# Four feed-forward stages of a hybrid decoder, issued in written order on every engine

## The chip, the cores and the metric

One core of one Trainium2 chip runs the whole program. The metric is the device time of one execution in microseconds (us); several runs are taken and their median is given. The profile comes from one further execution, with the hardware profiler on.

## What is computed

The input is 512 tokens of 1024 features in float32. Two layers follow one another, each a feed-forward block, a mixer (gated linear attention in the first layer, stick-breaking attention in the second) and another feed-forward block; a norm ends it. The change concerns the feed-forward blocks alone, of which there are four:

```
def rmsnorm(x, g):
    y = xf * lax.rsqrt(jnp.mean(xf * xf, axis=-1, keepdims=True) + EPS)
    return (y * g.astype(jnp.float32)).astype(x.dtype)

def swiglu(h, w_gate, w_up, w_down):
    return (jax.nn.silu(h @ w_gate) * (h @ w_up)) @ w_down

x = x + 0.5 * swiglu(rmsnorm(x, ffn1_norm[i]), ffn1_w_gate[i], ffn1_w_up[i], ffn1_w_down[i])
```

The gate and up weights are 1024 x 2816, the down weights 2816 x 1024.

## The kernel before

**Layout.** The residual stays in SBUF as eight tiles xs of 128 features x 512 tokens. Every float32 matrix product is made of three matmuls: each operand is cut into a high part (a cast by ScalarE, `wh`, `hh`, `nh`, `th`, `xh`) and a low part (VectorE subtracts the high part from the original: `wl`, `hl`, `nl`, `tl`, `xl`), and TensorE adds up high x high, high x low and low x high (`mm3`, L63 for the matmuls themselves).

**The feed.** All the work that needs weights stands in one list, `feed.q`, of entries. An entry has the weight units that it needs and a body with its matmuls and what empties them. `Feed.start` takes the next entry e. It first cuts the weights of e and of the entries behind it, up to three entries and four units of 128 x 1024 in all (`Entry.split`, cast in L134, subtraction in L135), then asks for the loads of e and the five entries behind it (SyncE, L114), then runs the body. `feed.entries(n)` starts n entries one after another. Of the cut weights there are four buffers each for high and low, of the loaded gate and up chunks (`raw`, 1 MB) two, of the loaded down chunks (`rawd`, 0.5 MB) two.

**A feed-forward stage** is one `FFN`. The 2816 columns are taken in 11 column blocks of 256 (c = 0 to 10), in six groups. Blocks 0 and 1 use plain products (`feat`), and so does the gate half of block 2. All others use a scheme of seven half-size products in place of eight (`seven`), which I call a block of seven products; each column block from 3 on has one for the gate weights and then one for the up weights. A block is two entries:

- `body_1` runs four products, into banks w, z, q and w again. Behind the first ScalarE copies w into `u` (L579). Behind the second VectorE adds z into `u` (L555), behind the third ScalarE copies q into `c` (L586), and behind the fourth the first half of an output o is made (`left`): by SiLU on ScalarE in a gate block, by a product with the gate on VectorE in an up block (L561).
- `body_2` runs three products, into the other half of z, onto q, and into the other half of w. VectorE adds (L555, L599); a gate block ends in two SiLUs (`rest`, L565), an up block in two products with the gate (L568), each of which is then cut into high and low for the down product (`close`: cast in L630, subtraction in L631).

The units of a block are partly sums of pieces of the loaded weights, made by VectorE while the weights are cut: two additions for `body_1` (`sums_12`, L529 and L530) and two for `body_2` (`sums_34`, L535 and L536). The programs below call all of these `s`.

Down entries (`down`, 24 matmuls each, emptied into xs by VectorE in L309) of the group before are put between the blocks: one behind each block of seven in column blocks 3 to 7, two in block 8, one each behind the up blocks of 9 and 10, and two ahead of the up block of 2. The last group's four come at the end.

At the start of a stage the plain entries are interleaved with `normed_input` (four pieces which scale, cut and difference the input) and then `sums` (eight pieces which cut the differences); `FFN.run` writes them between the calls of `feed.entries`.

**What sets the order.** The program is traced, and a scheduler at the end orders each engine's instructions by its own estimate of when they become ready, so an engine's queue can differ from the written order. Within `tc.manual_schedule()` it doesn't: there each engine issues in the order in which the program was written. Before the change only the opening of the whole kernel and a few lines of the first stage (L696 to L699) stand in such a block. An engine works through its queue in order either way: what is written behind a waiting instruction waits too. The data dependencies, the buffers and the waits for them are worked out by the framework for both.

Of the kernel before, what the change touches and what calls it, by code (L numbers as in the profile page):

```python
# [31 lines left out]
def decoder(ctx: ExitStack, tc: tile.TileContext, a: dict, out: bass.AP):  # L32
    nc = tc.nc
# [12 lines left out]
    def psum(name, tag=None):  # L46
        if tag is None:
            tag = order[turn_[0] % 8]
            turn_[0] += 1
        return pp.tile([P, T], F32, tag=tag, bufs=banks[tag], name=name)  # L50
# [11 lines left out]
    def mm(ps, l, r, first, last):  # L62
        st["pe"] = nc.tensor.matmul(ps, l, r, start=first, stop=last).ins  # L63
# [8 lines left out]
    def four(m):  # L72
        return m.rearrange("p (h t n) -> p t n h", h=2, t=2)
# [4 lines left out]
    def quads(ps):  # L78
        return ps.rearrange("p (t n h) -> p t n h", t=2, h=2)
# [99 lines left out]
    feed = Feed()  # L179
# [163 lines left out]
    st = {}  # L343
# [64 lines left out]
    def stats_b(tag=None, turned=False):  # L408

        ps = psum("ps_R", tag)  # L410
        dgs = sp.tile([P, T], F32, tag="ss", name="dg")
        for i in range(NT):
            dg = dgs[:, i * P : (i + 1) * P]
            nc.vector.tensor_scalar(
                out=dg, in0=ident, scalar1=st["r4"][:, i : i + 1], scalar2=None, op0=ALU.mult
            )
            mm(ps[:, i * P : (i + 1) * P], ones, dg, True, True)
        st["R"] = sp.tile([P, T], F32, tag="sq", name="R")
        nc.vector.tensor_copy(st["R"], ps)
        if turned:  # L420
            st["Rq"] = sp.tile([P, T], F32, tag="Rq", name="Rq")
            nc.vector.tensor_copy(quads(st["Rq"]), four(ps))

    def two_halves(between=None, n=2):

        feed.finish()
        g = [feed.start() for _ in range(n)]
        for i in range(3):
            for x in g:
                next(x, None)  # L430
            if i == 0 and between is not None:
                between()

    def new_norm():
        st["h"], st["l"] = st["nh"], st["nl"]

    def flush(deferred):
        for evac, ps in deferred:
            evac(ps)
        deferred.clear()  # L440
# [11 lines left out]
    class FFN:  # L452
# [235 lines left out]
        def run(self, between=None):  # L688
            with tc.tile_pool(name="hp", bufs=8, reuse_waits="tile") as self.hp, tc.tile_pool(
                name="tp", bufs=5, reuse_waits="tile"  # L690
            ) as self.tp:
                st["few"] = self.hp
                new_norm()

                if self.first:
                    with tc.manual_schedule():  # L696
                        feed.entries(1)
                        stats_b(turned=True)
                        flush(self.defer)  # L699
                else:  # L700
                    two_halves(stats_a)
                    stats_b(turned=True)
                    flush(self.defer)
                done = feed.pos - self.base
                for job, n in ((self.normed_input, self.NORMED - done), (self.sums, self.sums_by - self.NORMED)):
                    todo = list(job())
                    for i in range(n):
                        for piece in todo[i * len(todo) // n : (i + 1) * len(todo) // n]:
                            piece()
                        feed.entries(1)  # L710
                    self.normed = True
                    st["h"], st["l"] = zip(*self.n)
                feed.entries(self.count - self.sums_by)
                if between is not None:
                    with tc.issue_after(st["silu"]):
                        nc.scalar.preload_act_table_set("sqrt_and_others")
                    feed.q[feed.pos].split()
                    between(self.tp)
                feed.entries(self.total - self.count)


    class GLA:
# [764 lines left out]
```

## Time and profile before

| what | value |
|---|---|
| median of 3 runs | 1817.53 us (1817.35 to 1818.69) |
| the profiled execution: its time | 1816.56 us |
| the profiled execution: span from first to last instruction | 1814.8 us |
| busy share of TensorE, VectorE, ScalarE | 99%, 81%, 51% |
| mean granted TensorE clock | 0.998 |

The profile calls the engines PE (TensorE matmuls), PEld (TensorE weight loads), DVE (VectorE), ACT (ScalarE), POOL (GpSimd) and SP (SyncE). A row of a group names the line, the engine, the operation and the tiles as out<-in, with the numbers of buffers left out, then the count, the busy time, the mean duration of one, and the idle time of the engine ahead of them with what ended it. The four feed-forward stages lie at about 0 to 345, 575 to 907, 910 to 1235 and 1480 to 1815 us of the span; the two mixers between them.

### The profile page before, as it was taken

How to read it: one execution, taken by the hardware profiler on the slowest of the kernel's cores; microseconds unless marked ns; L12 is line 12 of the kernel's file. 1: busy time of each engine (PE TensorE's matmuls, PEld its weight loads, DVE VectorE, ACT ScalarE, POOL GpSimd, SP SyncE). 2: the span in 40 equal slices, each digit the busy share in tenths (PEclk: the TensorE clock that was granted, in tenths of full speed). 3: DMA queues.
4: the chain of work that ended last, by engine and by line, in shares of the span. 5: the costliest groups of instructions: out<-in, count | busy, mean ns of one | idle time of the engine just before them, and what ended most of it. 6: DMA issues, size and time to landing. Idle time of an engine off the chain costs nothing.

```text
span 1814.8 us, 28968 instructions
## 1 busy us (share of the span) xinstructions
PE 1794.2 (99%) x11806; PEld 1640.7 (90%) x11806; DVE 1473.1 (81%) x2373; ACT 926.2 (51%) x1455; POOL 8.5 (0%) x20
## 2 busy tenths in 40 slices
PE   9999999999999999999999999999999999999998
PEld 7899999889988899999989999999888788999997
DVE  7988887776877988887898888787888779888785
ACT  6444435445554544444554444455888844444444
POOL 0000000100000000000000000000000000000000
PEclk9999999999999999999999999999999999999999
DMA  6243333212223323332233333233221223333321
GB/s 210 72 131 112 105 117 114 84 51 67 70 70 102 107 94 112 113 125 84 82 119 119 110 116 106 89 96 96 70 71 59 70 93 116 105 105 105 120 90 70
DMA packets 177608, 179.09 MB, mean 99 GB/s; under 512 B 4098, under 2 KB 167988, under 8 KB 177476
## 3 DMA queue, kind: packets, MB, share of 16 engines
q1 hardware_dynamic: 176224, 175.13, 29.9%
q8 instruction: 92, 1.51, 0.3%
q0 software_dynamic: 576, 1.05, 0.2%
q10 hardware_dynamic: 676, 1.07, 0.2%
q14 instruction: 40, 0.33, 0.1%
HBM read 175.17 MB, written 2.10 MB: 98 GB/s over the span
## 4 chain that ended last, share of the span: by engine, by line
PE 85%; DVE 8%; ACT 4%; DMA 3%; issue 1%; DVEq 0%; ACTq 0%; SPq 0%
PE ps_d L63 23%; PE ps_w L544 14%; PE ps_f L63 14%; PE ps_z L544 9%; PE ps_q L544 9%; PE ps_t L63 4%; PE ps_b L63 3%; DVE wl L135 2%; PE ps_S L63 1%; DMA raw<-in_ffn_w_up_dram 1%; PE ps_bt L63 1%; PE ps_oT L1176 1%; PE ps_z L1114 1%; DMA raw<-in_ffn_w_gate_dram 1%; ACT wh L134 1%
## 5 line engine op out<-in xcount | busy, mean ns | idle before, releaser
L135 DVE TENSOR_TENSOR wl<-raw,wh 128x1024 fp32r<-128x1024 f32 x242 | 258.2, 1068 | 50.4 <-ACT wh L134 49.7
L134 ACT CAST wh<-raw 128x1024 fp32r<-128x1024 f32 (+1 forms) x242 | 223.8, 927 | 130.0 <-PE ps_f L63 43.4
L63 PE MATMUL ps_d<-hh,wh 128*128 128x512 f32 x672 | 254.7, 379 | 0.0
L63 PE MATMUL ps_d<-hh,wl 128*128 128x512 f32 x672 | 254.7, 379 | 0.0
L63 PE MATMUL ps_d<-hl,wh 128*128 128x512 f32 x672 | 254.7, 379 | 0.0
L134 ACT CAST wh<-s 128x1024 fp32r<-128x1024 f32 x136 | 142.3, 1046 | 115.0 <-PE ps_q L544 82.0
L135 DVE TENSOR_TENSOR wl<-s,wh 128x1024 fp32r<-128x1024 f32 x136 | 165.8, 1219 | 23.9 <-ACT wh L134 22.7
L63 PE MATMUL ps_f<-xh,wh 128*128 128x512 f32 x456 | 178.7, 392 | 3.4 <-DVE x L243 1.7
L63 PE MATMUL ps_f<-xh,wl 128*128 128x512 f32 x456 | 173.8, 381 | 0.4 <-DVE wl L1366 0.4
L63 PE MATMUL ps_f<-xl,wh 128*128 128x512 f32 x456 | 173.6, 381 | 0.0
L309 DVE SCALAR_TENSOR_TENSOR x<-ps_d,x 128x512 f32<-128x512 f32 x184 | 124.6, 685 | 59.8 <-PE ps_d L63 59.7
L544 PE MATMUL ps_z<-th,wh 128*128 128x256 f32 x544 | 150.1, 276 | 0.3 <-DVE u L555 0.2
L544 PE MATMUL ps_w<-nh,wl 128*128 128x256 f32 x544 | 149.6, 275 | 0.0
L544 PE MATMUL ps_w<-nl,wh 128*128 128x256 f32 x544 | 149.6, 275 | 0.0
L544 PE MATMUL ps_z<-th,wl 128*128 128x256 f32 x544 | 149.6, 275 | 0.0
L544 PE MATMUL ps_z<-tl,wh 128*128 128x256 f32 x544 | 149.6, 275 | 0.0
L544 PE MATMUL ps_w<-nh,wh 128*128 128x256 f32 x544 | 149.5, 275 | 0.0
L134 ACT CAST wh<-rawd 128x1024 fp32r<-128x1024 f32 x84 | 88.0, 1048 | 120.4 <-PE ps_d L63 100.7
L63 PEld LDWEIGHTS ps_d<-hl,wh 128*128 128x128 f32 x672 | 127.0, 189 | 18.0
L63 PEld LDWEIGHTS ps_d<-hh,wl 128*128 128x128 f32 x672 | 127.2, 189 | 16.5
L63 PEld LDWEIGHTS ps_d<-hh,wh 128*128 128x128 f32 x672 | 127.2, 189 | 16.5
L135 DVE TENSOR_TENSOR wl<-rawd,wh 128x1024 fp32r<-128x1024 f32 x84 | 102.6, 1222 | 34.7 <-ACT wh L134 34.4
(268 smaller groups left out, 4711.0 us busy)
## 6 DMA issues: line engine op xcount, KB each, us to landing
raw<-in_ffn_w_gate_dram SPq DMA_DIRECT2D x43, 1024.0 KB, 5.1
raw<-in_ffn_w_up_dram SPq DMA_DIRECT2D x43, 1024.0 KB, 5.1
rawd<-in_ffn_w_down_dram SPq DMA_DIRECT2D x84, 512.0 KB, 3.5
raw<-in_gla_w_in_dram SPq DMA_DIRECT2D x12, 1024.0 KB, 5.3
raw<-in_sb_w_in_dram SPq DMA_DIRECT2D x16, 512.0 KB, 3.8
raw<-in_gla_w_out_dram SPq DMA_DIRECT2D x4, 1024.0 KB, 5.1
raw<-in_sb_w_in_dram SPq DMA_DIRECT2D x4, 1024.0 KB, 5.0
raw<-in_sb_w_out_dram SPq DMA_DIRECT2D x4, 1024.0 KB, 4.9
```

Of the source, the lines that this page charges most:

```text
L63: st["pe"] = nc.tensor.matmul(ps, l, r, start=first, stop=last).ins
L134: nc.scalar.copy(h, r).ins,
L135: nc.vector.tensor_tensor(out=l, in0=r, in1=h.bitcast(F32), op=ALU.subtract).ins,
L309: nc.vector.scalar_tensor_tensor(out=x, in0=back_by(ps, 4), scalar=0.5, in1=x, op0=ALU.mult, op1=ALU.add)
L544: nc.tensor.matmul(pairs(o), l_, r_, start=first and j + n == 0, stop=j == 3 and n == 2, skip_group_check=True)
L1114: nc.tensor.matmul(o_, l_, r_, start=first, stop=last, skip_group_check=True)
L1176: nc.tensor.matmul(po[e * 64 : e * 64 + 64, j * P : T], self.v[j][:, c : c + 64], self.wt[p, e][bk][:, c0 : c0 + n], start=j == 0, stop=j ...
```

## The change

`FFN.run` now opens `tc.manual_schedule()` for the whole of the first stage, and in the other three from behind the first two entries and the norm; it is closed behind the last entry of the stage. In the last stage the load of the square-root table loses its `issue_after`, since the written order already puts it behind the last SiLU. Nothing is computed otherwise.

```
+                self.es = ExitStack()
                 if self.first:
-                    with tc.manual_schedule():
-                        feed.entries(1)
-                        stats_b(turned=True)
-                        flush(self.defer)
+                    self.es.enter_context(tc.manual_schedule())
+                    feed.entries(1)
+                    stats_b(turned=True)
+                    flush(self.defer)
                 else:
                     two_halves(stats_a)
                     stats_b(turned=True)
                     flush(self.defer)
+                    self.es.enter_context(tc.manual_schedule())
...
                 if between is not None:
-                    with tc.issue_after(st["silu"]):
-                        nc.scalar.preload_act_table_set("sqrt_and_others")
+                    nc.scalar.preload_act_table_set("sqrt_and_others")
                     feed.q[feed.pos].split()
                     between(self.tp)
                 feed.entries(self.total - self.count)
+                self.es.close()
```

The instructions of every engine are the same. TensorE's order differs at a few places, at the starts of the stages; that of VectorE and ScalarE differs all through the stages, that of SyncE a little.

First place: VectorE, an up block of seven products in the middle of the first stage, from the product with the gate (L561) to the second cut (L631). The o are the block's two outputs, u and c its helpers, s the sums of weights. Before:

```order
L561 TENSOR_TENSOR o_1785<-ps_w,o_1626 128x256
L135 TENSOR_TENSOR wl<-s_1844,wh 128x1024
L555 TENSOR_TENSOR o_1853<-ps_z,u_1798 128x256
L555 TENSOR_TENSOR o_1785<-ps_q,u_1798 128x256
L599 TENSOR_TENSOR o_1853<-o_1853,c_1825 128x256
L568 TENSOR_TENSOR o_1785<-o_1785,o_1626 128x256
L135 TENSOR_TENSOR wl<-s_1904,wh 128x1024
L631 TENSOR_TENSOR hl<-o_1785,hh 128x512
L555 TENSOR_TENSOR o_1853<-ps_w,o_1853 128x256
L135 TENSOR_TENSOR wl<-raw,wh 128x512
L568 TENSOR_TENSOR o_1853<-o_1853,o_1694 128x512
L309 SCALAR_TENSOR_TENSOR x_86<-ps_d,x_86 128x512
```

Now the same block, from the sums of the next weights on (the product with the gate and the wl of the raw weights stand just ahead):

```order
L529 TENSOR_TENSOR s_1843<-raw 128x512
L530 TENSOR_TENSOR s_1843<-s_1843,raw 128x512
L135 TENSOR_TENSOR wl<-s_1843,wh 128x1024
L555 TENSOR_TENSOR o_1852<-ps_z,u_1797 128x256
L599 TENSOR_TENSOR o_1852<-o_1852,c_1824 128x256
L555 TENSOR_TENSOR o_1784<-ps_q,u_1797 128x256
L568 TENSOR_TENSOR o_1784<-o_1784,o_1625 128x256
L631 TENSOR_TENSOR hl<-o_1784,hh 128x512
L555 TENSOR_TENSOR o_1852<-ps_w,o_1852 128x256
L568 TENSOR_TENSOR o_1852<-o_1852,o_1693 128x512
L631 TENSOR_TENSOR hl<-o_1852,hh 128x512
```

The sums are made directly ahead of the wl that needs them, where before they were made long before; and between each product with the gate (L568) and its hl (L631), with ScalarE's cast of the same o between them, nothing else stands any more.

Second place: VectorE, just behind that, up to the add into u (L555) of the following gate block, which reads bank z. Before:

```order
L309 SCALAR_TENSOR_TENSOR x_87<-ps_d,x_87 128x512
L135 TENSOR_TENSOR wl<-rawd,wh 128x1024
L529 TENSOR_TENSOR s_2170<-raw 128x512
L535 TENSOR_TENSOR s_2230<-raw 128x512
L555 TENSOR_TENSOR u_1965<-ps_z,u_1965 128x256
L530 TENSOR_TENSOR s_2170<-s_2170,raw 128x512
L536 TENSOR_TENSOR s_2230<-raw,s_2170 128x512
L135 TENSOR_TENSOR wl<-raw,wh 128x1024
L135 TENSOR_TENSOR wl<-s_2011,wh 128x1024
```

Now:

```order
L535 TENSOR_TENSOR s_1903<-raw 128x512
L536 TENSOR_TENSOR s_1903<-raw,s_1843 128x512
L135 TENSOR_TENSOR wl<-s_1903,wh 128x1024
L135 TENSOR_TENSOR wl<-raw,wh 128x512
L309 SCALAR_TENSOR_TENSOR x_86<-ps_d,x_86 128x512
L309 SCALAR_TENSOR_TENSOR x_87<-ps_d,x_87 128x512
L135 TENSOR_TENSOR wl<-rawd,wh 128x1024
L555 TENSOR_TENSOR u_1964<-ps_z,u_1964 128x256
L135 TENSOR_TENSOR wl<-raw,wh 128x1024
```

The whole cutting of the weights of the next `body_2`, both x of the down entry and the cutting of the next down weights now stand ahead of the add into u; before, sums of a later block's weights stood there, and those cuts were spread over the block.

## Prediction

> **What bounds the kernel now.** The page first. Columns: busy time, share of the span, instructions.
>
> ```profile
> PE 1794.2 (99%) x11806; PEld 1640.7 (90%) x11806; DVE 1473.1 (81%) x2373; ACT 926.2 (51%) x1455; POOL 8.5 (0%) x20
> ```
>
> TensorE has work nearly all the time, so at most 1814.8 - 1794.2 = 20.6 us can be won anywhere. The windows view says the same of the inside of a feed-forward stage (the second one here; columns: length, then busy time of PE, PEld, DVE, ACT, POOL, then clock, DMA share, GB/s):
>
> ```profile
> 640.00:860.00 220.00, 220.00 (x1627) 209.99 (x1626) 180.00 (x276) 98.48 (x142) 0.00 (x0) 1.00 0.32 104
> ```
>
> TensorE never pauses there, at full clock; VectorE is busy for 180 of 220 us. The chain of waits shows the period of that stage (start, length, work):
>
> ```profile
> 692.37 5.18 PE ps_d L63 x24
> 697.56 1.34 PE ps_w L544 x12
> 698.89 1.34 PE ps_z L544 x12
> 700.23 1.34 PE ps_q L544 x12
> 701.57 1.34 PE ps_w L544 x12
> 702.91 1.34 PE ps_z L544 x12
> 704.25 1.34 PE ps_q L544 x12
> 705.59 1.34 PE ps_w L544 x12
> ```
>
> One down entry (5.18 us) and one seven-product block (7 x 1.34 = 9.38 us): 14.56 us, with no gap. The first four products are body_1, the last three body_2. So this change can win almost nothing inside the four stages; what it can do is make TensorE wait. The question is whether VectorE and ScalarE, held to the written order, still deliver within 14.56 us.
>
> **The change part by part.** TensorE's order moves in a few places only, so its own work (1794.2 us) stays; no instruction is added or dropped, and the table load keeps its place behind the last SiLU. What moves is VectorE's and ScalarE's order, and a wait there now holds up everything written behind it. The prices of VectorE's and ScalarE's instructions in the second stage, by group (count | busy, mean ns | idle before, releaser):
>
> ```profile
> L135 DVE TENSOR_TENSOR wl<-s,wh 128x1024 fp32r<-128x1024 f32 x34 | 41.4, 1219 | 6.5 <-ACT wh L134 6.2
> L309 DVE SCALAR_TENSOR_TENSOR x<-ps_d,x 128x512 f32<-128x512 f32 x46 | 31.2, 685 | 15.0 <-PE ps_d L63 15.0
> L135 DVE TENSOR_TENSOR wl<-rawd,wh 128x1024 fp32r<-128x1024 f32 x22 | 26.9, 1221 | 9.1 <-ACT wh L134 9.0
> L536 DVE TENSOR_TENSOR s<-raw,s 128x512 f32<-128x512 f32 x17 | 11.7, 688 | 0.4
> L530 DVE TENSOR_TENSOR s<-s,raw 128x512 f32<-128x512 f32 x17 | 11.6, 681 | 0.0
> L135 DVE TENSOR_TENSOR wl<-raw,wh 128x512 fp32r<-128x512 f32 x17 | 11.6, 679 | 0.0
> L555 DVE TENSOR_TENSOR u<-ps_z,u 128x256 f32<-128x256 f32 x17 | 7.1, 419 | 2.5 <-PE ps_z L544 2.4
> L568 DVE TENSOR_TENSOR o<-o,o 128x512 f32<-128x512 f32 x8 | 5.5, 681 | 0.0
> L134 ACT CAST wh<-s 128x1024 fp32r<-128x1024 f32 x34 | 35.6, 1046 | 28.8 <-PE ps_q L544 20.5 <-PE ps_d L63 4.5 <-issue 3.7
> L630 ACT CAST hh<-o 128x512 fp32r<-128x512 f32 x18 | 11.2, 621 | 23.5 <-DVE o L568 23.4
> L579 ACT COPY u<-ps_w 128x256 f32<-128x256 f32 x17 | 6.4, 375 | 5.1 <-PE ps_w L544 4.9
> L565 ACT ACTIVATE o<-o 128x512 f32<-128x512 f32 x8 | 5.1, 633 | 4.9 <-DVE o L555 4.9
> ```
>
> And how they follow each other, in the timeline (start, duration):
>
> ```profile
> 189.77 0.27 PE L544 MATMUL ps_w<-nh,wh 128*128 128x256 f32 x1
> 189.97 0.69 DVE L309 SCALAR_TENSOR_TENSOR x<-ps_d,x 128x512 f32<-128x512 f32 x1 [1.90 <-PE ps_d L63]
> 198.34 0.41 DVE L555 TENSOR_TENSOR o<-ps_q,u 128x256 f32<-128x256 f32 x1
> 198.67 0.41 DVE L599 TENSOR_TENSOR o<-o,c 128x256 f32<-128x256 f32 x1
> 199.01 0.42 DVE L568 TENSOR_TENSOR o<-o,o 128x256 f32<-128x256 f32 x1
> 199.46 0.62 ACT L630 CAST hh<-o 128x512 fp32r<-128x512 f32 x1 [0.34 <-DVE o L568]
> 199.34 1.21 DVE L135 TENSOR_TENSOR wl<-s,wh 128x1024 fp32r<-128x1024 f32 x1
> 200.48 0.68 DVE L631 TENSOR_TENSOR hl<-o,hh 128x512 fp32r<-128x512 f32 x1
> 201.08 0.41 DVE L555 TENSOR_TENSOR o<-ps_w,o 128x256 f32<-128x256 f32 x1
> ```
>
> Independent instructions start 0.33 us (256 columns), 0.60 (512) and 1.14 (1024) apart, less than they last. A hand-over costs the full duration and 0.03 us (VectorE ends at 199.43, ScalarE starts at 199.46); I take the same for two dependent VectorE instructions in a row (0.45 us for 256 columns, 0.72 for 512). From TensorE's end, taken as the start of its next group, to VectorE it is 0.20 us (189.77 to 189.97). The last three rows show what the scheduler does: between the product o and its hl it has put a 1.14 us weight subtraction, so ScalarE's 0.62 us cast is hidden. The written order has nothing there.
>
> One round trip to ScalarE then costs VectorE 0.03 + 1.05 + 0.03, beside the lost overlap, behind each pair of weight sums (two per block), and 0.03 + 0.62 + 0.03 at each closing (two in a block of the up weights, none in one of the gate weights).
>
> Now the walk. Let L be the moment at which VectorE learns that body_1 of an up block has ended, with one down entry behind the block. In written order: product with the gate 0.33 and wl of the next weights 1.14 (its cast is done: its buffer came free one product earlier): L+1.47. Sums 0.72 + 0.72, cast 1.08, wl 1.14: 5.14. Three adds 0.45 + 0.33 + 0.45: 6.37. Product 0.45, cast 0.65, hl 0.60: 8.08. Add 0.45, product 0.72, cast 0.65, hl 0.60: 10.50. The other sums 0.60 + 0.72, cast 1.08, wl 1.14: 14.05. Small wl 0.60, two x 1.20, wl of the down weights 1.14: 16.99. Then the add into u, 0.42 + 0.04: 17.45. Who waits for that? The first product of body_2 writes the other half of the bank that this add reads:
>
> ```profile
> L544 PE MATMUL ps_z<-th,wh 128*128 128x256 f32 x544 | 150.1, 276 | 0.3 <-DVE u L555 0.2
> ```
>
> The wait exists today and costs nothing (0.2 us over 544 rows). TensorE alone would be at that product at L - 0.20 + 4.02 + 5.18 + 5.36 = L+14.36. It will stand for 17.45 - 14.36 = 3.1 us. ScalarE takes part of it: the small cast (0.62), the cast of the down weights (1.05) and the copy of u (0.38) follow the cast ending at L+12.88, so the fourth product, due at L+13.02, starts at 14.95. The gate block behind it has no closings: VectorE needs about 13.1 us and catches up, so the cost is per up block.
>
> Per stage: five such places (column blocks 3 to 7), 15.5 us. Behind column block 2 no down entry lies between its up block and the next gate block, so both weight splits stand ahead of the closings: from the same rows u is done at L+16.8 against L+9.2 due, 7.6 us. In the last two blocks the gate blocks are followed directly by up blocks: splits, adds, SiLU 0.63 and the cast of the down weights come before the copy of u; counted from the gate's body_2, 15.65 against 9.38 in one (6.3 us), and 1.7 less in the other, where VectorE is already late (4.6). Between those two pairs stands one up-to-gate place with a down entry of four x but no down-weight split: 3.1. Around block 8 two down entries cover the chain (L+19.5 against 19.5): 0. Sum: 15.5 + 7.6 + 6.3 + 4.6 + 3.1 = 37.1 us.
>
> The start of a stage is not in this pattern. The first stage has today's largest wait there:
>
> ```profile
> L63 PE MATMUL ps_f<-nh,wh 128*128 128x512 f32 x16 | 6.0, 386 | 1.4 <-ACT nh L630 1.4
> ```
>
> Four pieces that norm, split and difference the input (about 4.1 us of VectorE each by the widths above) now stand whole between the entries, with 0.6 to 2.7 us of eviction and a 1.14 us split, against 5.18 us of TensorE. TensorE is two entries behind the split, which absorbs most. Bounds: 2 us won in one stage (that wait gone) to 5 us lost; I take 2.5 lost in each. SyncE's loads stay in their order and move with the buffers, which now come free later:
>
> ```profile
> raw<-in_ffn_w_gate_dram SPq DMA_DIRECT2D x43, 1024.0 KB, 5.1
> ```
>
> By the walk the last read of a weight chunk lies about 20 us before the cast of the chunk that takes its buffer; 5.1 us of landing fit: nothing. The stage ends are taken at 0, at most 2 us each.
>
> Per stage 37.1 + 2.5 = 39.6 us, for four stages 158 us. The profiled execution took 1816.56 us (span 1814.8), 1 us under the median of the runs, 1817.53. Forecast: 1816.6 + 158 = **1975 us**.
>
> [...]
>
> **Rivals.** *No slower.* The four round trips per pair of blocks are 4 x 1.11 + 2 x 0.68 = 5.8 us, but only 3.47 of it lies in the chain from L to u. Were an up block's trips hidden, the chain would be 17.45 - 3.47 = 13.98, under the 14.36 that TensorE leaves, and nothing would stand. That needs ScalarE to have its casts done before VectorE arrives, which the data forbid for s and o. For it: 18% of VectorE is idle now. The time would be 1816.6, or up to 2 us less with the start's wait gone. Chance 0.07: 0.05 within 0.2%, 0.02 faster (0.2%, 3.6 us, is about what these runs can tell from no change).
>
> *VectorE's queue alone decides.* If TensorE's waits don't compound, only VectorE's total counts. For a pair of blocks: 180/220 x 29.12 = 23.8 of work, 5.8 of trips, 0.8 of lost overlap: 30.4 us against 29.12. Without downs 25.7 against 18.76. Blocks 2 and 3 then lose 6.9, 4 to 7 5.2, 9 and 10 12.2, and 8 gives back 4.4: 20 us a stage, 1896 us. Against it: VectorE stands idle at L until TensorE arrives. Chance 0.13.
>
> *The pauses cost clock as well.* The kernel's first matmuls, behind idle, ran slow:
>
> ```profile
> 1.50 3.48 PE ps_i L63 x8
> ```
>
> That is 435 ns each against 5.18/24 = 216, so 1.75 us lost in such a run-up. Three pauses a stage are long (7.6, 6.3, 4.6 us); twelve run-ups add 21 us: 1996 us. Against it: the pauses now in the kernel, up to 1.4 us in the row above, left no slow rows. Chance 0.18. [...]
>
> **How the numbers follow.** The forecast holds 0.62; the rest is above, so slower has 0.93. The low end is VectorE's queue alone less 6 us, 1890. The high end adds to the clock case the other bounds at the starts and ends (2.5 and 2 us, four times: 18 us) and 5% on a 17.45 us chain in about nine up blocks of which half of the excess shows (16 us): 2030.
>
> **What would show it.** Right: TensorE's busy time unchanged near 1794 us but its share near 91%; each stage about 40 us longer; the idle time before ps_z growing behind DVE u L555 and before ps_w behind ACT u L579, near 1.1 and 2.0 us at one block in two; wl from s idle about 1.1 us before each of its rows behind ACT wh, hl from o about 0.65. Periods alternate near 32.2 us per pair. Wrong: VectorE's idle time grows but ps_z doesn't wait (the no-slower case); waits at the matmuls for raw or rawd (then loads, which I price at nothing); a clock under 0.97.

## The result and the profile after

The changed kernel takes 2002.63 us (median of 4 runs, 2001.16 to 2003.3) against 1818.11 us for the kernel before on the same chip (4 runs, 1817.35 to 1820.13): a ratio of 1.1012, 95% interval 1.0993 to 1.1031. That is 184.5 us lost, where 158 were forecast. The profiled execution took 2003.3 us, with a span of 2001.5, so 186.7 us more span than before. The page of after, busy times first:

```profile
PE 1839.0 (92%) x11806; PEld 1667.4 (83%) x11806; DVE 1498.9 (75%) x2373; ACT 913.0 (46%) x1455; POOL 8.5 (0%) x20
```

TensorE does the same 11806 matmuls and is busy for 44.8 us more (1839.0 against 1794.2); the other 141.9 us are pauses. VectorE's share fell from 81% to 75% although it now sets the pace. The second feed-forward stage in the windows view, 220 us of it as before (length; busy time of PE, PEld, DVE, ACT, POOL; clock; DMA share; GB/s):

```profile
640.00:860.00 220.00, 199.54 (x1316) 184.12 (x1315) 170.30 (x258) 91.17 (x134) 0.00 (x0) 0.98 0.30 94
```

TensorE stands for 20.5 of 220 us where it never stood. What it stands for is in the groups (count | busy, mean ns | idle before, releaser):

```profile
L544 PE MATMUL ps_w<-nh,wh 128*128 128x256 f32 x544 | 159.0, 292 | 96.9 <-ACT u L579 96.9
L544 PE MATMUL ps_z<-th,wh 128*128 128x256 f32 x544 | 157.2, 289 | 32.6 <-DVE u L555 32.5
L135 DVE TENSOR_TENSOR wl<-s,wh 128x1024 fp32r<-128x1024 f32 x136 | 166.7, 1226 | 158.7 <-ACT wh L134 158.7
L631 DVE TENSOR_TENSOR hl<-o,hh 128x512 fp32r<-128x512 f32 x72 | 49.9, 693 | 49.3 <-ACT hh L630 49.3
```

The two rows of VectorE are the round trips: 158.7 us over 136 rows is 1.17 each, 49.3 over 72 is 0.68 each. The two rows of TensorE are the pauses that follow. One pair of blocks in the chain of waits (start, length, work), from the moment L at which VectorE learns that body_1 of an up block has ended:

```profile
798.37 0.03 DVE o L561
...
801.34 1.06 ACT wh L134
...
802.42 1.23 DVE wl L135
803.65 0.34 DVE o L555
...
805.27 0.63 ACT hh L630
...
805.92 0.69 DVE hl L631
...
807.71 0.63 ACT hh L630
...
808.36 0.69 DVE hl L631
...
810.37 1.06 ACT wh L134
...
811.45 0.56 DVE wl L135
...
815.61 0.34 DVE u L555
...
816.00 1.60 PE ps_z L544 x12
...
830.86 0.04 DVE o L561
```

From L = 798.37 the first add of body_2 starts in the chain at L+5.28, the second hl at L+9.99, and u is done at 815.61 + 0.34 = L+17.58. In the chain of before, TensorE followed TensorE at this place; here the thread goes from VectorE to ScalarE and back four times, and TensorE appears only when u is done. The next L comes at 830.86: a pair takes 32.49 us instead of 29.12. TensorE's pauses of one pair are in its timeline (start, duration, idle before):

```profile
780.72 0.38 PE L544 MATMUL ps_w<-nh,wh 128*128 128x256 f32 x1 [1.64 <-ACT u L579]
783.51 0.38 PE L544 MATMUL ps_z<-th,wh 128*128 128x256 f32 x1 [1.19 <-DVE u L555]
```

That is 2.83 us of pause; the rest of the 3.37 us lies behind the two pauses and is called the restart below (1.60 us for the twelve matmuls at 816.00, where they took 1.34 before). ScalarE's timeline has the reason for the first of the two, three casts ahead of the copy of u, the first of which waits for VectorE's sum s:

```profile
810.37 1.05 ACT L134 CAST wh<-s 128x1024 fp32r<-128x1024 f32 x1 [2.04 <-DVE s L536]
811.32 0.61 ACT L134 CAST wh<-raw 128x512 fp32r<-128x512 f32 x1
811.84 1.04 ACT L134 CAST wh<-rawd 128x1024 fp32r<-128x1024 f32 x1
812.79 0.36 ACT L579 COPY u<-ps_w 128x256 f32<-128x256 f32 x1
```

The longest pause lies behind column block 2, 7.26 us. Cut into stretches of 3.41 us, the windows view shows what happens to the clock there, and in the last three rows what happens around the two pauses above:

```profile
708.80:712.21 3.41, 0.00 (x0) 0.00 (x0) 2.66 (x7) 0.62 (x1) 0.00 (x0) 1.00 0.33 91
712.21:715.63 3.42, 0.07 (x1) 0.08 (x1) 2.45 (x5) 1.96 (x4) 0.00 (x0) 0.50 0.62 216
715.63:719.04 3.41, 3.41 (x16) 3.41 (x17) 1.19 (x2) 0.67 (x3) 0.00 (x0) 0.50 0.39 123
719.04:722.45 3.41, 3.41 (x33) 3.41 (x32) 2.52 (x3) 0.80 (x1) 0.00 (x0) 1.00 0.11 35
777.06:780.48 3.42, 2.02 (x19) 1.82 (x17) 2.23 (x4) 2.60 (x4) 0.00 (x0) 1.00 0.00 0
780.48:783.89 3.41, 1.99 (x15) 1.80 (x16) 3.16 (x6) 1.78 (x4) 0.00 (x0) 1.00 0.51 144
783.89:787.30 3.41, 3.41 (x33) 3.41 (x33) 2.34 (x3) 1.01 (x1) 0.00 (x0) 1.00 0.95 317
```

Behind the stretch in which TensorE stood idle (from 708.80) the clock is 0.50 for two stretches; in the first it runs one matmul, in the second it gets through 16 instead of 33. The short pauses of the steady pairs, 1.4 us of idle per stretch (from 777.06 and 780.48), were followed by a clock of 1.00. Over the whole span the mean granted clock is 0.983, so (1 - 0.983) x 2001.5 = 34.0 us of full clock are lost, against (1 - 0.998) x 1814.8 = 3.6 before.

### The profile page after: what moved, and what is told of

It reads as the page before. It is cut to its first block, busy times and chain, and to the rows that moved or that the text cites. A ratio compares the mean times of both kernels' runs of the same rounds, so it can differ in the third digit from the quotient of the medians.

```text
span 2001.5 us, 28971 instructions
## 1 busy us (share of the span) xinstructions
PE 1839.0 (92%) x11806; PEld 1667.4 (83%) x11806; DVE 1498.9 (75%) x2373; ACT 913.0 (46%) x1455; POOL 8.5 (0%) x20
## 3 DMA queue, kind: packets, MB, share of 16 engines
q0 software_dynamic: 576, 1.05, 0.2%
## 4 chain that ended last, share of the span: by engine, by line
PE 55%; DVE 29%; ACT 11%; issue 5%; DMA 1%; ACTq 0%; DVEq 0%
PE ps_d L63 12%; PE ps_f L63 11%; DVE wl L135 9%; PE ps_w L544 8%; ACT wh L134 6%; PE ps_z L544 5%; PE ps_q L544 5%; PE ps_t L63 4%; PE ps_b L63 3%; DVE x L309 2%; DVE hl L631 2%; ACT hh L630 2%; DVE o L555 2%; DVE o L568 2%; PE ps_S L63 1%
## 5 line engine op out<-in xcount | busy, mean ns | idle before, releaser
L135 DVE TENSOR_TENSOR wl<-s,wh 128x1024 fp32r<-128x1024 f32 x136 | 166.7, 1226 | 158.7 <-ACT wh L134 158.7
L544 PE MATMUL ps_w<-nh,wh 128*128 128x256 f32 x544 | 159.0, 292 | 96.9 <-ACT u L579 96.9
L134 ACT CAST wh<-raw 128x1024 fp32r<-128x1024 f32 x242 | 222.7, 924 | 49.0 <-PE ps_f L63 20.3
L544 PEld LDWEIGHTS ps_w<-nh,wh 128*128 128x128 f32 x544 | 108.9, 200 | 105.3 <-ACT u L579 103.8
L544 PE MATMUL ps_z<-th,wh 128*128 128x256 f32 x544 | 157.2, 289 | 32.6 <-DVE u L555 32.5
L544 PE MATMUL ps_z<-th,wl 128*128 128x256 f32 x544 | 154.1, 283 | 3.0 <-DVE wl L135 3.0
L544 PE MATMUL ps_w<-nl,wh 128*128 128x256 f32 x544 | 155.5, 286 | 0.0
L544 PE MATMUL ps_w<-nh,wl 128*128 128x256 f32 x544 | 155.2, 285 | 0.0
L544 PEld LDWEIGHTS ps_z<-th,wh 128*128 128x128 f32 x544 | 109.1, 201 | 37.8 <-DVE u L555 37.4
L630 ACT CAST hh<-o 128x512 fp32r<-128x512 f32 x72 | 44.5, 618 | 182.1 <-DVE o L568 182.1
```

The source lines that it names most:

```text
L134: nc.scalar.copy(h, r).ins,
L135: nc.vector.tensor_tensor(out=l, in0=r, in1=h.bitcast(F32), op=ALU.subtract).ins,
L544: nc.tensor.matmul(pairs(o), l_, r_, start=first and j + n == 0, stop=j == 3 and n == 2, skip_group_check=True)
L630: nc.scalar.copy(h, t)
```

## The experiments

Theory: VectorE in written order stands through every round trip to ScalarE, the chain from L to u gets longer than TensorE's work, and TensorE pauses at ps_w and ps_z; the long pauses cost clock on top. Rivals: ScalarE's order by itself; the order of the loads or of TensorE; VectorE's total of work rather than its chain. Times stand against runs of the kernel before that were taken beside them (medians of 1817.9 to 1819.0 us).

### Which engine's order it is

One engine each, or a group, is held to the written order, and the others are left to the scheduler. The edit for VectorE (the others name Activation, or PE, SP and Pool); the first lines of the first stage keep the form that they had in before:

```
-                    self.es.enter_context(tc.manual_schedule())
+                self.es.enter_context(tc.manual_schedule(engines={mybir.EngineType.DVE}))
```

**VectorE alone.**

> Only VectorE is held to the written order in the four stages; ScalarE, TensorE, SyncE and GpSimd are left to the scheduler. Theory (VectorE's chain decides, ScalarE only hands casts over): most of the 185 us stays. What ScalarE can give back is the pause at ps_w (1.65 us at five places in each of four stages, at most 33 us, if u is copied ahead of the casts); the pause at ps_z stays. Expected 1965 to 2003 us, waits of wl from s behind ACT wh still about 1.1 us each. Rival (ScalarE's order decides, by the copies of u that stand behind casts): 1817 to 1850 us. Rival (both orders are needed together): about half, near 1910 us.

Measured: 1919.16 us, ratio 1.0554 (1.0539 to 1.0570), 101 us lost. TensorE's waits:

```profile
PE ps_f L63 <- DVE wl L135: 16.2, 12, 3.2
PE ps_w L544 <- ACT u L579: 10.7, 12, 1.5
PE ps_z L544 <- DVE u L555: 9.8, 24, 0.6
```

The round trips are all there (wl from s still stands 158.4 us behind ACT wh), but with ScalarE free to copy u ahead of casts the waits at ps_w fall from 96.9 to 10.7 us, and those at ps_z from 32.5 to 9.8. The theory as put, that ScalarE only hands over and most of the 185 us stays, falls: 55% stays. The number is that of the second rival.

**ScalarE alone.**

> Only ScalarE is held to the written order. Theory: ScalarE has 46% of the span to do, and its casts come no later than their inputs, which VectorE, in the scheduler's order, brings as early as before; a copy of u behind a cast can cost up to 1 us at some blocks. Expected 1817 to 1850 us. Rival (ScalarE's order decides): above 1950 us. Rival (both orders are needed together): near 1910 us.

Measured: 1886.62 us, ratio 1.0383 (1.0350 to 1.0417), 68 us lost. Every theory missed, the first by 37 us. TensorE's and VectorE's timelines around one of its pauses:

```profile
751.18 0.69 DVE L135 TENSOR_TENSOR wl<-raw,wh 128x512 fp32r<-128x512 f32 x1
...
757.45 0.69 DVE L529 TENSOR_TENSOR s<-raw 128x512 f32<-128x512 f32 x1 [3.51 <-DMA raw<-in_ffn_w_up_dram]
758.06 0.69 DVE L535 TENSOR_TENSOR s<-raw 128x512 f32<-128x512 f32 x1
758.66 0.42 DVE L561 TENSOR_TENSOR o<-ps_w,o 128x256 f32<-128x256 f32 x1
```

```profile
759.13 0.38 PE L544 MATMUL ps_w<-th,wh 128*128 128x256 f32 x1 [2.10 <-DVE o L561]
```

And the load between them in the chain of waits:

```profile
751.90 5.53 DMA raw<-in_ffn_w_up_dram
```

This is another loss than in the fully ordered kernel, whose VectorE has no such DMA wait. (In the kernel before, such waits last at most 1.6 us.) The wl behind ScalarE's small cast reads the chunk until 751.87, only then does the next load into that buffer begin, and VectorE, whose first sums the scheduler has put ahead of the product with the gate (L561), stands 3.51 us for it.

**The same without most of those loads.**

```
-                        g, u = Chunk(cols(wg, c * 256, 256), KD, 256), Chunk(cols(wu, c * 256, 256), KD, 256)
+                        if c < 4:
+                            g, u = Chunk(cols(wg, c * 256, 256), KD, 256), Chunk(cols(wu, c * 256, 256), KD, 256)
```

> Only ScalarE is held to the written order, and from column block 4 of each stage on the gate and up weights of block 3 are used again instead of new ones (56 loads of 1 MB are left out, and the result is that of other weights; every product, sum and cast is still done). Theory (in the kernel with ScalarE's order alone, 1886.6 us, the small cast of a chunk comes late, so the next load into that buffer is issued late, VectorE's first sum of a split stands up to 4.7 us for it, and TensorE waits about 2 us for the product with the gate behind that sum, once in two blocks): without those loads most of the 68 us goes, 1817 to 1845 us; the scheduler may place VectorE's work otherwise. Rival (ScalarE's order costs through late casts alone, not through loads): 1870 to 1890 us.

Measured: 1842.57 us, ratio 1.0133 (1.0118 to 1.0148): 44 of the 68 us are gone, and no wait at ps_w is left among the longest. That is as the theory had it. The scheduler placed VectorE's work otherwise once the loads were gone, so the size is not the loads' alone. The two single losses, 101 and 68 us, happen to add to 169 of 184.5, but the second is of another kind, so this is no sum of parts.

**TensorE, SyncE and GpSimd.**

> Only TensorE, SyncE and GpSimd are held to the written order. Theory: TensorE's order moves in a few places and SyncE's loads stay in sequence, so 1815 to 1822 us, no pause over 2 us inside a stage. Rival (the loads or TensorE's order make the loss): above 1900 us. Rival (a small part, at the stages' starts and ends): 1823 to 1840 us.

Measured: 1818.3 us (10 runs), ratio 1.0001 (0.9992 to 1.0011). The order of TensorE and of the loads costs nothing. One pause is over the 2 us of the expectation, 2.23 us at the start of the first stage.

**One stage alone**, with the written order on all engines where the stage's number is that of the second:

```
-                    self.es.enter_context(tc.manual_schedule())
+                    if self.gi == 4:
+                        self.es.enter_context(tc.manual_schedule())
```

> All engines are held to the written order in the second of the four stages alone. Theory (each stage loses by itself, about 46 us of the 185 us): 1817.5 + 46 = 1864 us, with the same pauses in that stage as in the fully ordered kernel (7.3 us behind block 2, pairs of 1.65 and 1.19 us, 4.6 and 4.0 us at blocks 9 and 10) and three half-clock windows in it. Rival (the loss carries over, a stage that starts late makes the next one later, or the mixture of stages costs more): over 1885 us. Rival (most of the loss lies in the first or last stage): under 1850 us.

Measured: 1865.99 us, ratio 1.0261 (1.0245 to 1.0276), 47.6 us; four times that is 191 against 184.5. TensorE's waits there (us, times, longest; 96.9 us in 36 and 32.5 in 24 over all four stages of after):

```profile
PE ps_w L544 <- ACT u L579: 25.0, 9, 7.3
PE ps_z L544 <- DVE u L555: 9.9, 9, 2.2
```

So the second stage loses its quarter by itself, and no loss that is carried over shows; the other three were not run alone.

### Filling the round trips

The subtractions that follow a cast are put on a list and written down later: closings one product later (the lines below), weights one after each product or part of a down entry; where both are put off, one of the list follows each product. What is still on the list from before when the next entry begins is written there.

```
+    def cut_low(l, r, h):
+        def sub():
+            nc.vector.tensor_tensor(out=l, in0=r, in1=h.bitcast(F32), op=ALU.subtract)
+        late.append(sub) if st["pipe"] else sub()
...
+            held = 0
             for _ in range(n):
                 for _ in self.start():
-                    pass
+                    pop(held)
+                    held = len(late)
```

**Closings (hl) alone.**

> The ordered kernel, with each hl subtraction of a closing written one product later, so that VectorE has other work while ScalarE casts; weight subtractions stay as they are. Theory (the chain of 17.45 us overshoots TensorE's 14.36 us by what the round trips cost; two closings' trips of 0.65 us are in it): the 3.3 us lost per pair of blocks shrinks by 1.3 us, and so do the long pauses; with 20 pairs and 12 longer places 32 x 1.3 = 42 us less: about 1960 us. Rival (only VectorE's total of work counts): the same 2 x 0.68 us of idle in every up block, 36 of them, 49 us less: 1953 us, not told apart. Rival (the weights' trips alone matter): 1995 to 2003 us.

Measured: 1960.52 us, ratio 1.0774 (1.0758 to 1.0790), 42 us less than after, as worked out. The groups of VectorE and TensorE:

```profile
L147 DVE TENSOR_TENSOR wl<-s,wh 128x1024 fp32r<-128x1024 f32 x136 | 166.7, 1225 | 158.8 <-ACT wh L146 158.8
L121 DVE TENSOR_TENSOR hl<-o,hh 128x512 fp32r<-128x512 f32 x72 | 49.3, 684 | 0.1
L560 PE MATMUL ps_w<-nh,wh 128*128 128x256 f32 x544 | 158.0, 290 | 59.9 <-ACT u L595 59.9
```

The closings' trips are gone (0.1 us over 72), the weights' are untouched, and in the steady pairs only one pause of 1.56 us, at ps_z, remains.

**Weights (wl) alone.** The same list, taking the wl subtractions and not hl.

> The ordered kernel, with each wl subtraction of a weight split written later (one after each product or part of a down entry), so that VectorE has other work while ScalarE casts; closings stay as they are. Theory (two of the weights' trips of 1.11 us lie in the chain, and the lost overlap beside them): 17.45 - 2.2 = 15.2 us against 14.36, so the 3.3 us lost per pair shrink to about 0.9 us, 20 x 2.4 = 48 us less, at the twelve longer places about 3 us each, 36 us less, and of the half-clock windows about half go, 15 us: about 1900 us (1860 to 1925). Rival (only VectorE's idle total counts, 4 x 1.11 us per pair): about 1850 us. Rival (the closings' trips are what holds TensorE): above 1970 us.

Measured: 1895.76 us, ratio 1.0423 (1.0407 to 1.0438), 107 us less than after. The groups:

```profile
L121 DVE TENSOR_TENSOR wl<-s,wh 128x1024 fp32r<-128x1024 f32 x136 | 166.0, 1220 | 27.7 <-ACT wh L145 27.7
L643 DVE TENSOR_TENSOR hl<-o,hh 128x512 fp32r<-128x512 f32 x72 | 49.9, 692 | 49.3 <-ACT hh L642 49.3
```

Two pauses of 0.46 and 0.59 us are left in a steady pair, 1.05 against the 0.9 expected for the pair.

**Both.**

> The ordered kernel with both kinds of subtraction written later, so that no instruction of VectorE directly follows the cast it needs. Theory: the chain falls to about 17.45 - 3.47 = 13.98 us, under the 14.36 us that TensorE leaves, so the steady pauses go: 1815 to 1835 us, what is left being the places without a down entry (behind block 2, blocks 9 and 10). Rival (a written order loses to the scheduler for other reasons, for instance VectorE's queue waiting for TensorE in turn): above 1880 us. Rival (the effects don't add: one of the two kinds alone was enough): the same time as with that kind alone.

Measured: 1847.64 us, ratio 1.0160 (1.0143 to 1.0177), 155 us less than after; the two single gains add to 149. The groups, then the second stage in the windows view:

```profile
L121 DVE TENSOR_TENSOR wl<-s,wh 128x1024 fp32r<-128x1024 f32 x136 | 165.4, 1216 | 0.0
L121 DVE TENSOR_TENSOR hl<-o,hh 128x512 fp32r<-128x512 f32 x72 | 47.0, 685 | 0.4
```

```profile
640.00:860.00 220.00, 217.72 (x1569) 206.24 (x1568) 178.52 (x271) 95.91 (x139) 0.00 (x0) 1.00 0.33 103
```

Not one trip is waited for, TensorE has its 220 us back but for 2.3 at the first seven-product block, and the steady pairs have no pause. The time is 13 us over the range of the theory: of the 29 us that it still loses, 14.5 are waits of ps_f for wl, most of them at the stages' starts, where the deferred wl now comes too late (7.8 us in after), and about 9 lie at the four first seven-product blocks. Blocks 9 and 10, which the theory had named, have no pause.

**Both, with VectorE alone in that order.**

> The kernel with both kinds of subtraction written later (1847.6 us), with VectorE alone held to that order and the other engines left to the scheduler. Theory (what is left of the loss, 29 us, lies in ScalarE's written order and at the stages' starts, where TensorE waits for wl): ScalarE's part goes, 1820 to 1835 us. Rival (what is left is VectorE's order alone): 1843 to 1852 us. Rival (the written VectorE order is better than the scheduler's once its round trips are filled): under 1815 us.

Measured: 1847.22 us, ratio 1.0163 (1.0148 to 1.0178). The theory missed and the first rival holds: freeing ScalarE gives back nothing. So VectorE's order alone is enough for the rest of the loss, and once its trips are filled ScalarE's written order costs nothing more. No version tried beats the kernel before.

### Which work sets the pace

Three more instructions of the same add, in the body_2 of the up blocks or of the gate blocks (4 and 1 change places):

```
-                nc.vector.tensor_tensor(out=o1[:, H:T], in0=u3, in1=v["c5"], op=ALU.add)
+                for _ in range(4 if group is not None else 1):
+                    nc.vector.tensor_tensor(out=o1[:, H:T], in0=u3, in1=v["c5"], op=ALU.add)
```

**In the up blocks.**

> The ordered kernel with one add of 256 columns of each up block's body_2 done four times (the same result, three more instructions of 0.33 us, 1.0 us in all, in VectorE's chain from L to u). Theory (in up blocks the chain sets TensorE's pace one for one): 1.0 us more at each of the eight up blocks of a stage whose chain is late (all seven-product ones but block 8), 32 us, and up to 10 us more where pauses now reach a half-clock window: 2030 to 2047 us. Rival (only the total of VectorE's work counts, 82% of the time in the pair): 2003 to 2015 us, as in the gate blocks.

Measured: 2075.69 us (2049.23 to 2079.76), ratio 1.1382 (1.1298 to 1.1466), 73 us over after where 32 to 42 were expected, and less steady than any other kernel here. VectorE's timeline, then TensorE's:

```profile
827.29 1.80 DVE L600 TENSOR_TENSOR o<-o,c 128x256 f32<-128x256 f32 x4
829.01 0.41 DVE L555 TENSOR_TENSOR o<-ps_q,u 128x256 f32<-128x256 f32 x1
```

```profile
141.26 0.38 PE L544 MATMUL ps_w<-nh,wh 128*128 128x256 f32 x1 [3.03 <-ACT u L579]
...
175.13 0.38 PE L544 MATMUL ps_w<-nh,wh 128*128 128x256 f32 x1 [3.03 <-ACT u L579]
```

The four adds take 829.01 - 827.29 = 1.72 us where one takes 0.34, so 1.38 us were added, not 1.0: three more that write the same half of one tile are 0.46 us apart, like a dependent pair of that size in after (0.45 us, L555 at 803.57 and L599 at 804.02). The two rows of TensorE are one pair apart, 33.87 us for the 32.49 of after, and the pause at ps_w is 3.03 for 1.65: 1.38 us, one for one. No half clock is drawn in these first pairs of the first stage. In 17 of the 20 pairs the longer pause is followed by half clock. At block 2 the pause grows alike (8.63 for 7.26 in the second stage), at blocks 9 and 10 it doesn't (4.64 and 4.02), so the eight places of the expectation were too many. Over the whole kernel the waits at ps_w grow by 36.5 us (133.4 for 96.9) and those at ps_z shrink by 9.5 (23.0 for 32.5). The larger part of the 73 us is clock: TensorE is busy for 42.1 us more (1881.1 for 1839.0), and the mean clock falls to 0.957, which is 89 us of full clock lost against 34, some of it in the pauses.

**In the gate blocks.**

> The same three added instructions (1.0 us) in the body_2 of each gate block instead. Theory (VectorE catches up in the gate block and then stands 1.44 us for TensorE ahead of L, so 1.0 us has room): no change at the five steady pairs of a stage; only blocks 2, 9 and 10, without a down entry between gate and up or between up and gate, can lose, up to 2 x 1.0 us per stage: 2002 to 2012 us. Rival (VectorE's total of work sets the pace): the same as with the work in the up blocks, 2030 us and more.

Measured: 2021.19 us, ratio 1.1115 (1.1098 to 1.1132), 18.6 us over after and 54.5 below the same work in the up blocks. TensorE's timeline, first in a steady pair up to the next, then at block 9 (4.64 us in after):

```profile
786.78 0.38 PE L544 MATMUL ps_w<-nh,wh 128*128 128x256 f32 x1 [1.33 <-ACT u L579]
789.57 0.38 PE L544 MATMUL ps_z<-th,wh 128*128 128x256 f32 x1 [1.19 <-DVE u L555]
...
819.25 0.38 PE L544 MATMUL ps_w<-nh,wh 128*128 128x256 f32 x1 [1.33 <-ACT u L579]
...
941.99 0.58 PE L544 MATMUL ps_w<-nh,wh 128*128 128x256 f32 x1 [6.02 <-ACT u L579]
```

In the steady pairs the pauses did not grow, and a pair takes 32.47 us (786.78 to 819.25) for the 32.49 of after. In this stage the pauses at blocks 9 and 10 grow by 1.38 us each (6.02 for 4.64, 5.40 for 4.02), of which 1.30 come back between the two, where one pause of 1.54 us stands for 0.65 and 2.19. Over the whole kernel the waits hardly change (95.9 us for 96.9 at ps_w, 34.5 for 32.5 at ps_z), and TensorE is busy for 14.6 us more (1853.6 for 1839.0): most of the 18.6 us is clock, whose mean is 0.976, 48.5 us lost against 34.0. Neither number of the expectation was met: the expected 2012 us is passed by 9 us, and the 2030 us of the rival are not reached. So in the steady pairs it is the chain that sets the pace, not the total of VectorE's work.

### What the lost clock is worth

Extra matmuls of 256 columns fill the three long pauses of each stage:

```
+        FILL = {(3, False): 60, (9, True): 38, (10, True): 32}
...
+                for _ in range(self.fill):
+                    nc.tensor.matmul(
+                        pairs(v["q"][:, H:T]), s[0][:, 0], bh, start=False, stop=False, skip_group_check=True
+                    )
```

> The ordered kernel with extra matmuls of 256 columns, whose result is used by nothing, put on TensorE where its three long pauses of each stage lie (60, 38 and 32 of them, 0.11 us each: 6.7, 4.3 and 3.6 us against pauses of 7.3, 4.6 and 4.0 us). Theory (pauses of 4 us and more are followed by a window of half clock, 4 of 6.83 us and 7 of 3.41 us at these places, half of each lost, together 26 us): those windows go and the time falls to about 1977 us (1970 to 1990). Rival (the slow matmuls behind a pause cost nothing, since VectorE sets the pace there): 2000 to 2010 us. Rival (the extra matmuls themselves overrun the pauses): above 2010 us.

Measured: 1989.69 us, ratio 1.0931 (1.0912 to 1.0951): 13 us back, at the upper edge of what the theory gave. The page:

```profile
PE 1882.8 (95%) x12326; PEld 1712.9 (86%) x12326; DVE 1498.4 (75%) x2373; ACT 913.3 (46%) x1455; POOL 8.5 (0%) x20
```

Of the busy time 520 x 0.112 = 58.2 us (1.34 us for twelve) are the extra matmuls; the others take 1824.6 us, 14.4 less than in after. The mean clock is 0.993, 13.9 us lost instead of 34.0. I had counted half of each half-clock stretch; the first of the two behind block 2 lies almost wholly in the pause itself and costs nothing, and pauses of 1.9 and 2.2 us that stayed unfilled drew half clock here in stretches where they had not in after: outside the filled pauses after loses 6.4 us (1.7 each behind 50.02, 408.42 and 1330.02 us, 1.2 at the end), of the 13.9 lost here.

## Why the prediction was right, and where it was short

The sign, the place and the mechanism were right, and the time lies in the range; the forecast itself is 28 us short.

**The chain.** This part was worked out, not lucky. Each step of the walk holds within 0.2 us: u was due at L+17.45 and is done at L+17.58; a pair was to take about 32.2 us and takes 32.49. Of the 3.1 us pause, about 2.0 were given to ps_w and 1.1 to ps_z; 1.64 and 1.19 were measured, with 0.26 us of restart behind each. Doing the walk with durations of rows and 0.03 us per hand-over was enough.

**The places.** Idle before the matmul, in the second stage: 7.26 us behind block 2 (7.6 forecast), 0.75 + 4.64 at block 9 (6.3), 0.65 + 2.19 between up 9 and gate 10 (3.1), 4.02 at block 10 (4.6), 1.90 at the start (2.5), none around block 8 (0). These and the five pairs are 35.6 us; with 0.26 us of restart behind each of the 17 pauses that is 40.0, where 39.6 were forecast. That it is so close is partly luck: the pairs cost more (3.35 for 3.1), blocks 2, 9 and 10 less, and the 2.5 us at the start were a choice between two bounds.

**"TensorE's busy time unchanged near 1794 us."** This step failed: it is 1839.0. The forecast's sum has no term for the clock, and the pauses cost clock as well, the case that had been set aside as a rival at 0.18, with twelve run-ups and 21 us, 1996 us in all. That is 7 us short where the forecast is 28 short: of the named cases, this one came closest. Three places a stage did draw half clock, as named there; the mean clock fell by 0.015, and filling the three pauses brought back 13 us. In the half-clock stretches of after TensorE is busy for 51.8 us (3.4 in before), and half of that, 25.9 us (1.7), is lost; together with the restarts, 0.26 us at some 70 added pauses or 18 us, that is 42 of the 44.8 us. What spoke against that rival, that the pauses of the kernel before left no slow rows, was read too narrowly. It looked at pauses up to 1.4 us, where the pauses forecast were 4.6 to 7.6 us long; and the trace of before does have one stretch of half clock in which TensorE works, from 359.72 to 363.13 us, behind a pause of 1.60 us in the first mixer.

**ScalarE.** Its share of the chain was in the walk, but the walk treated it as following VectorE. With VectorE alone in order 83 of the 184.5 us go, and 86 us of waits at ps_w with them. The order of TensorE, SyncE and GpSimd alone costs nothing, so these 83 us are put down to ScalarE's order, as long as the trips are unfilled. That it is the place of the copy of u is read from the waits; no run moved that copy alone. And the step "loads: nothing" held for this change (the order of SyncE and TensorE alone has the ratio 1.0001, and VectorE in after waits for no such load), though not for ScalarE's order alone.

**Per up block, not per gate block.** The extra adds show it: a pair takes 1.38 us more for 1.38 in the up blocks, and no more for the same in the steady gate blocks. The rival in which VectorE's queue alone decides (1896 us) is out by that, as is the one without loss: the round trips are visible in after, and gone with the loss when other work is written into them.

**Not settled.** The 29 us left when all trips are filled were followed only to waits at the stages' starts (14.5 us) and first seven-product blocks (about 9 us); no run took them away.

## What to carry to other kernels

When a scheduler's order is replaced by a written one, look for instructions that stand directly behind another engine's answer to them: each cost VectorE the whole round trip here (1.17 us at a wl, 0.68 at an hl), and the hl subtractions written one product later cost next to nothing (0.1 us over 72 rows). Occupancy didn't show this (VectorE's share fell from 81% to 75%); walk the longest chain through one period with row durations and hand-overs and compare it with what the pacing engine needs in that period. Then look how long each pause of TensorE will be: the eleven of 4.02 to 7.26 us in after were all paid a second time in clock, those of 2 to 3 us by where they fell (one of the four of 2.19 us in after, 17 of the 20 of 3.0 us with more work in the up blocks).

## What the runs showed of the hardware

The half-clock stretches of one execution all begin on one grid of 3.41 us (in after at 50.02, 101.22 and 323.09 us, 15 and then 65 steps on), at a phase that differs between the two kernels' executions: counted from the span's start 2.24 us in after, 1.31 in before. The stretches of both spans along these grids, the last 10 us left aside, by TensorE's idle time in each: in after 17 have 2.05 us of idle or more, and all were followed by half clock; nine have 1.79 to 1.90 us, and one was (1.90 us from 46.61, while 1.87 us from 661.01 was not); 82 have 0.3 to 1.75 us, and one was (1.70 us from 405.01). In before the largest has 1.71 us, from 356.30, and was followed by half clock; 13 more with 0.3 to 1.5 us were not. With less than 0.3 us none was, of 474 in after and 514 in before. So a pause of 2 to 3 us lost clock or not by where it fell on the grid. In after the 2.19 us at 1327.80 lie whole in one stretch, and half clock followed; of those at 341.88, 953.03 and 1942.87 no stretch holds more than 1.81 us, and they lost none. The 3.03 us pauses of the first three pairs in the run with more work in the up blocks, of which no stretch holds more than 1.85 us, lost none, where the other 17 did. The eleven pauses of 4.02 to 7.26 us in after were all followed by half clock. The two pauses of 1.64 and 1.19 us of a steady pair, which never put more than 1.81 us into one stretch, drew no half clock in any of the 20 pairs of after.

A second finding: VectorE instructions that write the same half of one tile, and read its other half, followed one another 0.46 us apart (1.38 us for three, at 827.29 in the run with more work in the up blocks), against 0.33 for independent ones of that size (198.34 and 198.67 in before). Whether the chip or a wait that the framework put between them makes the difference was not tested.
